# Two score maps in one visit, two value chunks in one visit: a paged decode woven into the dense products of a hybrid decoder step

## The chip, the cores and the metric

The kernel runs on one core of a Trainium2 chip. Time is the device time of the whole program in microseconds (us); less is better. TensorE (PE) does matrix products and transposes, VectorE (DVE) and ScalarE (ACT) elementwise work, GpSimd (POOL) issues the gathers from the page pool, SyncE (SP) most other DMAs. The activations, the weights and the caches come from device memory at the start, and all results are written there.

## The reference

One layer of a decoder for 2048 prompt tokens and for 8 samples of 8 new tokens that each have 8192 cached ones. One projection feeds a gated short convolution and a differential attention; both go through one output projection, and a squared-ReLU MLP follows. The part that the change touches is the attention of the samples over the paged cache:

```python
def sample_attention(q, k, v, lam, k_pool, v_pool, page_table):
    kp = k_pool[page_table].reshape(bd, past, N_HEADS, 2, D_HEAD)    # 8 x 8192 x 4 x 2 x 64
    vp = v_pool[page_table].reshape(bd, past, N_HEADS, D_V)          # 8 x 8192 x 4 x 128
    return diff_attn(q, cat(kp, k), cat(vp, v), past + arange(tn), arange(past + tn), lam)

def diff_attn(q, k, v, q_pos, k_pos, lam):
    s = einsum('bqhcd,bkhcd->bchqk', q, k) * D_HEAD ** -0.5          # c: two score maps
    s = where(dist >= 0, s - slope * dist, NEG)
    p = softmax(s)
    return einsum('bhqk,bkhd->bqhd', p[:, 0] - lam * p[:, 1], v)
```

## The kernel before

**Dense work.** The input projection, the attention of the prompt, the output projection and the MLP are products of 128 x 128 weights with up to 512 columns. Each is made from three passes over split operands (`mm3`, L199 to L201, and L1410 to L1412 for the second MLP product), so three matmuls on TensorE belong together. After such a trio the code calls `between(us)` (L176), the place where other work may be put in.

**Decode.** `decode()` (from L685) is a generator that does the samples' attention in small steps. `tick(us)` (L167) adds the dense work's time to `since` and to a credit, and takes the next step when the credit is positive and `since` has reached the gap that the last step asked for, times 0.7. Each `yield cost, gap` in the generator ends a step. A step's instructions on TensorE, a **visit**, stand thus together between two dense trios. TensorE, like every engine, works through its instructions in the order of the program.

**Rounds.** `rounds()` (from L869) walks over the batches in two phases: the first 2 samples within the input projection (113 to 611 us of the trace), the other 6 within the output projection and the MLP (from about 1143 to 2219 us). A round takes a pair of chunks, 2 x 512 tokens; a sample has 8 rounds. The scores of a round belong to sample b, its values to sample b - 1, so the first 8 rounds of a phase have no values and the last 8, its tail, no keys. In order, a round is:

- scores `sps` (L896 to L908): two maps c, 8 products each of the block-diagonal queries `qbd` with the transposed keys `kt` (16 records in the trace); one step for each map; then DVE adds the bias and takes the maximum (L910);
- `more(n)`: n of the eight transposes of the next round's keys from `kraw` to `kt` on DVE (L717); behind the fourth and the eighth of them (L720 to L723) `gather_k` issues the gather of a later chunk (1 MB, L699); 5 of the 8 stand here, 2 and 1 behind the next steps;
- the exponentials of a round of sample b - 1, the transposes `pps` (L937) of its probabilities, their copies `ptt` on ACT (L940);
- values `o_ps` (L943 to L955): two chunks e, 16 products each (32 records), one step for each chunk; after a chunk's products `gather_v` (L702) issues four gathers of 256 KB for the chunk after next into the buffer `vpg` that this chunk has used. There are two such buffers.

`GP` and `GP2` hold the gaps of a round, for phase one and phase two: `(3, 2, 1, 3, 2, 2, 3, 3)` and `(2, 1, 2, 3, 2, 2, 3, 3)`; `gp()[1]` stands behind the first map, `gp()[0]` behind the second, `gp()[2]` behind the exponentials, `gp()[3]` behind the copies and `gp()[4]`, `gp()[5]` behind the two value chunks. In the code `gp()` takes GP where `b0` is zero. All gathers go through GpSimd's queue in the order in which the code issues them.

Of the kernel before, what the change touches and what calls it, by code (L numbers as in the profile page):

```python
# [20 lines left out]
EPS = 1e-5  # L21
# [45 lines left out]
def tile_hymba_step(  # L67
# [8 lines left out]
    T = x_prompt.shape[1]  # L76
# [59 lines left out]
    def rsqrt(y, v, n, w, eng=None):  # L136
        """y[:n, :w] = v ** -0.5 by Newton's iteration from the exponent trick."""
# [38 lines left out]
    def between(us):  # L176
        """A place between two products where other work of the tensor engine may go."""
        if fillers:
            fillers.pop(0)()
        else:  # L180
            tick(us)
# [15 lines left out]
    def mm3(ps, wh, wl, ah, al, first, last):  # L197
        """ps += (wh + wl)^T (ah + al), all but the product of the two low parts."""
        nc.tensor.matmul(ps, lhsT=wh, rhs=ah, start=first, stop=False)  # L199
        nc.tensor.matmul(ps, lhsT=wh, rhs=al, start=False, stop=False)  # L200
        nc.tensor.matmul(ps, lhsT=wl, rhs=ah, start=False, stop=last)  # L201

    class Weights:
        """Streams [128, 1024] weight tiles and splits each into two float32r parts, ahead of use."""
# [29 lines left out]
        def parts(self):  # L234
            """Closures that split the next tile, a half at a time."""
# [26 lines left out]
        def ahead(self, n):  # L262
            """Splits the next n tiles after those taken."""
# [7 lines left out]
    def norm_sum(x, n, junk=None):  # L271
        """The mean square of each row of x[:n]."""
# [6 lines left out]
    def norm_root(ss, n, eng=None):  # L279
        """(ss + EPS) ** -0.5 for one value a row."""  # L280
# [23 lines left out]
    # order of the column groups of w_in: Q, K, V, then (C, U, B) per convolution group  # L304
# [5 lines left out]
    # the last block ends with Q, whose results leave without a transpose  # L310
# [4 lines left out]
    # token tiles of each block in two chunks of columns: (source, first row, rows, column)  # L315
# [28 lines left out]
    def prep_sum(bi, ci, ss, i):  # L344
        """Sums of squares of a tile of tokens."""
# [17 lines left out]
    def prep_scale(bi, ci, rr):  # L363
        """Closures that normalise a chunk's tokens."""
# [7 lines left out]
    def trans(bi, ci):  # L372
        """Closures that transpose and split a chunk's tokens."""
# [29 lines left out]
    # the first tile's norm by itself  # L403
# [42 lines left out]
    class Proj:  # L446
        """One column group of w_in for one block of tokens."""
# [163 lines left out]
    def proj2(bi, mi):  # L611
        """Two column groups, chunk by chunk: at the ends of a block, where the activations change."""
# [58 lines left out]
    def row_fold(dst, src, op):  # L671
        """dst[(h,g,q), c] = over g: op of src[(h,g,q), c]."""
# [10 lines left out]
    def decode():  # L683
# [28 lines left out]
        def transpose_k(r, t, k):  # L712
            """An eighth of the transposed keys of a pair of chunks."""
# [11 lines left out]
        def load_qc(j):  # L725
            """Queries of four batches."""
# [13 lines left out]
        # page rows: keys in rows of 32 groups of four tokens, values token by token  # L740
# [9 lines left out]
        # bias of a cached key: slope (key - end of its pair of chunks) + slope (that end - query)  # L750
# [31 lines left out]
        # a page's scores and values have token 4 s + j in row 32 j + s  # L782
# [3 lines left out]
        # rows of the scores: (head, page in the group of four, token of the sample)  # L786
# [13 lines left out]
        # lambda on every partition  # L800
# [6 lines left out]
        # rows of the output: (head, map, token) in the first 16 of each 32  # L807
# [7 lines left out]
        # new tokens: column s of group g is token 32 g + s = (batch 4 g + s // 8, s % 8)  # L815
        # distance t - q; allowed where it is not positive
        nc.vector.tensor_scalar(scr[:, 0, :], scr[:, 0, :], rowf[:, 0:1], None, op0=ALU.subtract)
        # owner batch of the column, for this row's group
# [17 lines left out]
        # collects rows (h, c, q) into columns (h, q)  # L836
# [13 lines left out]
        def exps(b, k):  # L850
            """Exponentials of a batch's eighth k of the cached keys; NPR: of the new keys."""
# [8 lines left out]
        def more(n):  # L860
            """Some more of the next pair's transposed keys."""
# [6 lines left out]
        def rounds():  # L868
            """The pairs of chunks of batches b0 to b1."""  # L869
# [14 lines left out]
            for r in range(b0 * NPR, N_PR + NPR):  # L884
# [3 lines left out]
                if r < N_PR:  # L888
# [7 lines left out]
                    # scores of this pair of chunks of four pages  # L896
                    sps = dps.tile([P, 2, 256], F32, tag="sps", bufs=DPB - 1, name="sps")
                    for c in range(2):
# [9 lines left out]
                        yield 1.05, gp()[0] if c else gp()[1]  # L908
# [10 lines left out]
                if pb >= 0:  # L919
# [23 lines left out]
                    yield 0.4, gp()[3]  # L943
                    for e in range(2):
# [10 lines left out]
                        if it + 2 < b1 * NCH:  # L955
                            gather_v(it + 2)
                        more(MO[3 + e])
                        yield 1.2, gp()[4 + e]
# [80 lines left out]
        # sub-norm of the sample tokens: sums over the partitions by a product with ones  # L1039
# [59 lines left out]
    # units in groups of about four chunks of keys  # L1099
# [9 lines left out]
    # loads by the iteration after which they are issued  # L1109
# [11 lines left out]
    def attention_first():  # L1121
        """The attention's first tiles, ahead of the input projection's end."""
# [7 lines left out]
        # key - query position for the last query block; masked past the diagonal  # L1130
# [1021 lines left out]
```

## Time and profile before

| | |
|---|---|
| device time, median of 3 runs (range) | 3255.04 us (3251.31 to 3256.69) |
| span of the profiled execution | 3153.6 us |
| between the median and that span | 101.4 us |
| TensorE busy | 3014.2 us (96%) |
| VectorE / ScalarE / GpSimd busy | 58% / 39% / 28% |
| decode on TensorE, first to last | 112.9 to 2217 us, with a pause for the prompt's attention |

The profile is of one execution; the results give no device time for it besides its span, so the span stands for it and the 101.4 us are what lies around it. A timeline row tells the start, the length and the form of an instruction or of a run of like ones; matmuls overlap, so a group's cost is read from start to start, not from the sum of lengths. In the records a value product of the code stands as two, and so does a score product. An idle time in brackets names what ended it.

### The profile page before, as it was taken

The page shows a single profiled execution, that of the slowest core. Times are in us where ns is not written, and L with a number is a line of the kernel's source. Part 1 is how long each engine was busy: PE and PEld are TensorE (multiplying, and loading weights), DVE is VectorE, ACT ScalarE, POOL GpSimd, SP SyncE. Part 2 cuts the span into 40 slices and gives each one's busy share as a digit, 9 for nine tenths or more (in the row PEclk, how much of TensorE's full clock was granted, in tenths as well). Part 3 has the DMA queues.
Part 4 walks back from the last instruction along what each step waited for, and adds up shares of the span by engine and source line. Part 5 has one row for each costly group of instructions (what it writes and reads, how often), then busy time and mean ns, then how long its engine had stood idle before and what let it go on. Part 6 is the DMA issues. An engine that isn't in the chain of part 4 may idle for free. (4 is left out here: it accounts for less than half of the span.)

```text
span 3153.6 us, 53285 instructions
## 1 busy us (share of the span) xinstructions
PE 3014.2 (96%) x20902; PEld 2532.3 (80%) x20902; DVE 1824.8 (58%) x3751; ACT 1243.3 (39%) x2705; POOL 891.8 (28%) x1266
## 2 busy tenths in 40 slices
PE   7999998999999989999999999999999999999998
PEld 7988887989997788777677777777887788888886
DVE  5376353268888668766676776663653444444444
ACT  3323323357778643333343333343332332222222
POOL 0013355211122121455466564467002010000002
PEclk9999999999999999999999999999999999999999
DMA  4777876754335457899689899677741112111111
GB/s 149 229 232 247 286 255 200 223 140 113 108 99 146 139 176 242 278 320 334 229 288 360 304 347 328 211 274 263 230 145 41 61 54 67 47 54 47 54 47 64
DMA packets 400821, 585.80 MB, mean 186 GB/s; under 512 B 35413, under 2 KB 299605, under 8 KB 384186
## 3 DMA queue, kind: packets, MB, share of 16 engines
q1 hardware_dynamic: 337418, 301.07, 31.1%
q0 software_dynamic: 61984, 277.91, 24.5%
q8 instruction: 165, 2.70, 0.3%
q10 hardware_dynamic: 1168, 3.41, 0.3%
q14 instruction: 86, 0.70, 0.1%
HBM read 526.56 MB, written 55.74 MB: 185 GB/s over the span
## 5 line engine op out<-in xcount | busy, mean ns | idle before, releaser
L707 POOL DMA_INDIRECT vpg<-in_cache_v_dram,pt x512 | 537.5, 1050 | 232.3 <-issue 134.4
L226 ACT CAST wh<-wraw 128x1024 fp32r<-128x1024 f32 x336 | 350.0, 1048 | 632.2 <-PE dps L1412 277.1
L228 DVE TENSOR_TENSOR wl<-wraw,wh 128x1024 fp32r<-128x1024 f32 x336 | 410.2, 1221 | 236.4 <-ACT wh L226 227.4
L199 PE MATMUL ups<-h2h,wh 128*128 128x384 f32 (+2 forms) x1264 | 462.6, 366 | 4.9 <-DVE x L1417 2.5
L1417 DVE TENSOR_TENSOR x<-dps,x 128x512 f32<-128x512 f32 (+1 forms) x528 | 355.2, 684 | 177.2 <-PE dps L1412 176.7
L1410 PE MATMUL dps<-wh,uh 128*128 128x512 f32 (+1 forms) x1076 | 438.8, 408 | 13.2 <-ACT wh L226 5.6
L201 PE MATMUL ups<-h2h,wl 128*128 128x384 f32 (+2 forms) x1264 | 448.8, 355 | 0.0
L200 PE MATMUL ups<-h2l,wh 128*128 128x384 f32 (+2 forms) x1264 | 447.9, 354 | 0.0
L1411 PE MATMUL dps<-wl,uh 128*128 128x512 f32 (+1 forms) x1076 | 425.5, 395 | 4.3 <-DVE wl L228 3.3
L1412 PE MATMUL dps<-wh,ul 128*128 128x512 f32 (+1 forms) x1076 | 424.2, 394 | 0.0
L199 PE MATMUL ps<-hh,wh 128*128 128x384 f32 (+1 forms) x1152 | 404.6, 351 | 1.1 <-ACT cc L1526 0.7
L201 PE MATMUL ps<-hh,wl 128*128 128x384 f32 (+1 forms) x1152 | 376.5, 327 | 3.1 <-DVE wl L228 3.1
L200 PE MATMUL ps<-hl,wh 128*128 128x384 f32 (+1 forms) x1152 | 376.0, 326 | 0.1
L1369 DVE TENSOR_TENSOR ul<-r,uh 128x384 fp32r<-128x384 f32 (+2 forms) x158 | 93.6, 592 | 438.5 <-ACT uh L1368 438.3
L717 DVE STREAM_TRANSPOSE kt<-kraw 128x512 f32<-128x512 f32 x512 | 316.9, 678 | 5.4 <-DMA kraw<-in_cache_k_dram,idxk 5.4
L699 POOL DMA_INDIRECT kraw<-in_cache_k_dram,idxk x128 | 129.1, 1009 | 565.6 <-DVE kt L717 522.8
L199 PEld LDWEIGHTS ups<-h2h,wh 128*128 128x128 f32 x1264 | 238.5, 189 | 54.4 <-issue 28.7
L1410 PEld LDWEIGHTS dps<-wh,uh 128*128 128x128 f32 (+1 forms) x1076 | 200.8, 187 | 85.8 <-issue 24.1
L1366 ACT ACTIVATE r<-ups 128x384 f32<-128x384 f32 (+2 forms) x158 | 82.8, 524 | 445.0 <-PE ups L201 445.0
L200 PEld LDWEIGHTS ups<-h2l,wh 128*128 128x128 f32 x1264 | 238.9, 189 | 16.6
L201 PEld LDWEIGHTS ups<-h2h,wl 128*128 128x128 f32 x1264 | 238.5, 189 | 15.3
L284 POOL TENSOR_SCALAR ss<-ss 128x1 f32<-128x1 f32 (+1 forms) x33 | 9.5, 289 | 839.5 <-ACT junk L276 838.7
(275 smaller groups left out, 4985.8 us busy)
## 6 DMA issues: line engine op xcount, KB each, us to landing
wraw<-in_w_up_dram SPq DMA_DIRECT2D x128, 512.0 KB, 5.0
wraw<-in_w_down_dram SPq DMA_DIRECT2D x128, 512.0 KB, 3.3
wraw<-in_w_in_dram SPq DMA_DIRECT2D x72, 512.0 KB, 4.4
wraw<-in_w_out_dram SPq DMA_DIRECT2D x32, 512.0 KB, 4.2
x<-in_x_prompt_dram SPq DMA_DIRECT2D x24, 512.0 KB, 7.0
vpg<-in_cache_v_dram,pt POOLq DMA_INDIRECT x512
qt<-QH SPq DMA_DIRECT2D x64, 128.0 KB, 4.5
qt<-QL SPq DMA_DIRECT2D x64, 128.0 KB, 5.0
```

The source lines that it names most:

```text
L199: nc.tensor.matmul(ps, lhsT=wh, rhs=ah, start=first, stop=False)
L200: nc.tensor.matmul(ps, lhsT=wh, rhs=al, start=False, stop=False)
L201: nc.tensor.matmul(ps, lhsT=wl, rhs=ah, start=False, stop=last)
L226: nc.scalar.copy(wh, t)
L228: eng.tensor_sub(wl, t, wh.bitcast(F32))
L699: nc.gpsimd.indirect_dma_start(out=t.rearrange("p a b -> p (a b)"), out_offset=None, in_=ck, in_offset=bass.IndirectOffsetOnAxis(ap=idxk[: ...
L707: nc.gpsimd.indirect_dma_start(out=t[:, g, :], out_offset=None, in_=cv, in_offset=bass.IndirectOffsetOnAxis(ap=idxv[:, 4 * it + g:4 * it + ...
L717: nc.vector.transpose(t[:, e, 16 * j:16 * j + 16].rearrange("p a b -> p (a b)"), kraw[2 * r + e][:, 16 * j:16 * j + 16].rearrange("p a b - ...
L1410: nc.tensor.matmul(ps, lhsT=uh, rhs=wh[:, half], start=(i == 0), stop=False)
L1411: nc.tensor.matmul(ps, lhsT=uh, rhs=wl[:, half], start=False, stop=False)
L1412: nc.tensor.matmul(ps, lhsT=ul, rhs=wh[:, half], start=False, stop=(i == len(ms) - 1))
L1417: nc.vector.tensor_add(xx, ps, xx)
```

## The change

The two maps of a round's scores are made in one step with the gap that stood behind the second; the gap that stood behind the first is added to the one ahead of the values. The two chunks of values are made in one step with the sum of their gaps; their gathers are issued behind both. The rest of the diff takes comments away; line numbers from L956 on are higher by one after it.

```diff
                     for c in range(2):
                         for db in range(2):
...
-                        yield 1.05, gp()[0] if c else gp()[1]
+                    yield 2.1, gp()[0]
...
                     more(MO[2])
-                    yield 0.4, gp()[3]
+                    yield 0.4, gp()[3] + gp()[1]
                     for e in range(2):
                         it = NCH * pb + 2 * i + e
                         v = vpg.pop(it)
...
-                        if it + 2 < b1 * NCH:
-                            gather_v(it + 2)
+                    for e in range(2):
+                        if NCH * pb + 2 * i + e + 2 < b1 * NCH:
+                            gather_v(NCH * pb + 2 * i + e + 2)
                         more(MO[3 + e])
-                        yield 1.2, gp()[4 + e]
+                    yield 2.4, gp()[4] + gp()[5]
```

How the instructions stand then is shown at three places. The first is TensorE at the scores of one round of phase two, whose keys are `kt` and queries `qbd`; `dps` is a dense product of the MLP. Before:

```order
L902 MATMUL sps_15857<-kt_15729,qbd_14450 32x256 x8
L1410 MATMUL dps_15852<-wh_15717,uh_15527 128x512
L1411 MATMUL dps_15852<-wl_15718,uh_15527 128x512
L1412 MATMUL dps_15852<-wh_15717,ul_15528 128x512
L1410 MATMUL dps_15870<-wh_15640,uh_15450 128x512
L1411 MATMUL dps_15870<-wl_15641,uh_15450 128x512
L1412 MATMUL dps_15870<-wh_15640,ul_15451 128x512
L902 MATMUL sps_15857<-kt_15729,qbd_14450 32x256 x8
```

The same scores after:

```order
L1412 MATMUL dps_15716<-wl_15582,uh_15373 128x512
L1413 MATMUL dps_15716<-wh_15581,ul_15374 128x512
L902 MATMUL sps_15724<-kt_15599,qbd_14368 32x256 x16
L1411 MATMUL dps_15742<-wh_15483,uh_15293 128x512
L1412 MATMUL dps_15742<-wl_15484,uh_15293 128x512
L1413 MATMUL dps_15742<-wh_15483,ul_15294 128x512
```

The two visits with two dense trios between them have become one visit of 16 products.

The second place is TensorE at the values of a round of phase two; `ptt` holds the probabilities, `vpg` the gathered values of one chunk, and `ps` and `ups` are dense. Before:

```order
L949 MATMUL o_ps_13174<-vpg_14918,ptt_15055 16x128 x16
L1410 MATMUL dps_15105<-wh_14858,uh_14651 128x512
L1411 MATMUL dps_15105<-wl_14859,uh_14651 128x512
L1412 MATMUL dps_15105<-wh_14858,ul_14652 128x512
L1410 MATMUL dps_15105<-wh_14930,uh_14714 128x512
L1411 MATMUL dps_15105<-wl_14931,uh_14714 128x512
L1412 MATMUL dps_15105<-wh_14930,ul_14715 128x512
L199 MATMUL ups_15119<-h2h00_12958,wh_15019 128x384
L200 MATMUL ups_15119<-h2l00_12960,wh_15019 128x384
L201 MATMUL ups_15119<-h2h00_12958,wl_15020 128x384
L949 MATMUL o_ps_13174<-vpg_14962,ptt_15055 16x128 x16
```

The same values after:

```order
L200 MATMUL ups_14949<-h2l01_12961,wh_14823 128x384
L201 MATMUL ups_14949<-h2h01_12959,wl_14824 128x384
L949 MATMUL o_ps_13174<-vpg_14861,ptt_14963 16x128 x16
L949 MATMUL o_ps_13174<-vpg_14866,ptt_14963 16x128 x16
L199 MATMUL ups_15042<-h2h00_12958,wh_14913 128x384
L200 MATMUL ups_15042<-h2l00_12960,wh_14913 128x384
```

The products of the second chunk follow those of the first, and the three dense trios that stood between them stand outside.

The third place is GpSimd's queue in a round of phase two, its two key gathers and the first six of its eight value gathers, with the engines and DMA queues that an instruction waits for (PE is TensorE, DVE VectorE, DMASW a queue of gathers). Before:

```order
L699 DMA kraw<-in_cache_k_dram,idxk 128x2048 [waits DMASW4_49,DVE_49]
L699 DMA kraw<-in_cache_k_dram,idxk 128x2048 [waits DMASW5_49,DVE_49]
L707 DMA vpg<-in_cache_v_dram,pt 128x512 [waits DMASW7_49,DMASW6_49,PE_49]
L707 DMA vpg<-in_cache_v_dram,pt 128x512
L707 DMA vpg<-in_cache_v_dram,pt 128x512 [waits DMASW0_49]
L707 DMA vpg<-in_cache_v_dram,pt 128x512 [waits DMASW1_49]
L707 DMA vpg<-in_cache_v_dram,pt 128x512 [waits DMASW3_49,DMASW2_49,PE_49]
L707 DMA vpg<-in_cache_v_dram,pt 128x512
```

And after:

```order
L699 DMA kraw<-in_cache_k_dram,idxk 128x2048 [waits DMASW2_49,DVE_49]
L699 DMA kraw<-in_cache_k_dram,idxk 128x2048 [waits DMASW3_49,DVE_49]
L707 DMA vpg<-in_cache_v_dram,pt 128x512 [waits DMASW5_49,DMASW4_49,PE_49]
L707 DMA vpg<-in_cache_v_dram,pt 128x512
L707 DMA vpg<-in_cache_v_dram,pt 128x512 [waits DMASW6_49]
L707 DMA vpg<-in_cache_v_dram,pt 128x512 [waits DMASW7_49]
L707 DMA vpg<-in_cache_v_dram,pt 128x512 [waits DMASW1_49,DMASW0_49,PE_49]
L707 DMA vpg<-in_cache_v_dram,pt 128x512
```

The order and the kinds of the waits are the same: two key gathers that wait for DVE, then the value gathers, of which the first and the fifth wait for PE. What moved is TensorE's instruction behind which these waits end.

## Rows read from the trace of the kernel before

**Rows 1.** Page, part 1: busy time, share of the span, instructions of each engine.

```profile
PE 3014.2 (96%) x20902; PEld 2532.3 (80%) x20902; DVE 1824.8 (58%) x3751; ACT 1243.3 (39%) x2705; POOL 891.8 (28%) x1266
```

**Rows 2.** Tile answers, score and value products: ns min/median/max, first and last start, forms.

```profile
L902 PE MATMUL sps<-kt,qbd x2048: 376/379/637, 112.9 to 2092.7; 128*32 128x256 f32 x187
...
L949 PE MATMUL o_ps<-vpg,ptt x4096: 269/273/421, 299.9 to 2211.8; 128*16 128x128 f32 x196
```

**Rows 3.** Timeline of TensorE, one score visit: start us, us, operation, tile, count.

```profile
1301.12 0.33 PE L200 MATMUL ups<-h2l,wh 128*128 128x384 f32 x1
1301.29 0.34 PE L201 MATMUL ups<-h2h,wl 128*128 128x384 f32 x1
1301.56 1.07 PE L902 MATMUL sps<-kt,qbd 128*32 128x256 f32 x16
...
1302.85 0.34 PE L200 MATMUL ups<-h2l,wh 128*128 128x384 f32 x1
```

**Rows 4.** Timeline of TensorE, one value visit.

```profile
2012.34 0.34 PE L201 MATMUL ups<-h2h,wl 128*128 128x384 f32 x1
2012.61 1.07 PE L949 MATMUL o_ps<-vpg,ptt 128*16 128x128 f32 x32
...
2013.88 0.34 PE L200 MATMUL ups<-h2l,wh 128*128 128x384 f32 x1
```

**Rows 5.** Waits of TensorE, whole span: us in total, times, longest.

```profile
PE o_ps L949 <- DMA vpg<-in_cache_v_dram,pt: 20.7, 25, 2.3
...
PE o_ps L949 <- ACT ptt L940: 13.3, 6, 5.0
```

**Rows 6.** Timeline of GpSimd's queue in the second tail; in brackets the idle time before.

```profile
2123.23 0.98 POOL L707 DMA_INDIRECT vpg<-in_cache_v_dram,pt  x1 [6.40 <-PE o_ps L949]
...
2133.34 1.43 POOL L707 DMA_INDIRECT vpg<-in_cache_v_dram,pt  x1 [0.30 <-issue]
```

**Rows 7.** Timeline of TensorE in the same tail, value visits of two rounds.

```profile
2121.86 1.07 PE L949 MATMUL o_ps<-vpg,ptt 128*16 128x128 f32 x32
...
2132.15 1.07 PE L949 MATMUL o_ps<-vpg,ptt 128*16 128x128 f32 x32
...
2135.62 0.41 PE L949 MATMUL o_ps<-vpg,ptt 128*16 128x128 f32 x8
...
2139.09 0.63 PE L949 MATMUL o_ps<-vpg,ptt 128*16 128x128 f32 x8 [1.85 <-DMA vpg<-in_cache_v_dram,pt]
```

**Rows 8.** Timeline of TensorE, rounds with key gathers: two score visits, one late value group.

```profile
1727.07 1.07 PE L902 MATMUL sps<-kt,qbd 128*32 128x256 f32 x16
...
1755.26 0.41 PE L949 MATMUL o_ps<-vpg,ptt 128*16 128x128 f32 x8 [1.29 <-DMA vpg<-in_cache_v_dram,pt]
...
1822.17 1.07 PE L902 MATMUL sps<-kt,qbd 128*32 128x256 f32 x16
```

**Rows 9.** Timeline of GpSimd's queue in the same two rounds.

```profile
1741.83 0.94 POOL L699 DMA_INDIRECT kraw<-in_cache_k_dram,idxk  x1 [2.03 <-DVE kt L717]
1743.08 1.61 POOL L707 DMA_INDIRECT vpg<-in_cache_v_dram,pt  x1 [0.30 <-issue]
...
1747.50 0.95 POOL L707 DMA_INDIRECT vpg<-in_cache_v_dram,pt  x1 [0.30 <-issue]
...
1752.50 1.00 POOL L707 DMA_INDIRECT vpg<-in_cache_v_dram,pt  x1 [0.31 <-issue]
...
1830.67 1.92 POOL L699 DMA_INDIRECT kraw<-in_cache_k_dram,idxk  x1 [0.30 <-issue]
```

**Rows 10.** Windows: us, busy PE, PEld, DVE, ACT, POOL, granted clock, DMA share, GB/s.

```profile
1700.00:1930.00 230.00, 226.66 (x2162) 174.21 (x2164) 167.41 (x319) 86.86 (x181) 140.27 (x133) 1.00 0.94 332
...
2139.50:2142.50 3.00, 3.00 (x13) 2.33 (x8) 1.16 (x2) 0.00 (x0) 2.17 (x3) 0.55 0.72 246
```

**Rows 11.** Waits of TensorE between 2096 and 2215 us, the second tail.

```profile
PE o_ps L949 <- DMA vpg<-in_cache_v_dram,pt: 6.0, 7, 1.9
```

**Rows 12.** Waits of TensorE between 1200 and 2090 us, phase two with key gathers.

```profile
PE o_ps L949 <- DMA vpg<-in_cache_v_dram,pt: 8.5, 11, 1.5
```

## The prediction, made before the changed kernel ran

> **What bounds the kernel now.** I read the page's table of busy times first: TensorE is busy 3014.2 of 3153.6 us, 96%, and the next engine, VectorE, 58% [rows 1]. So a microsecond taken from TensorE's own work is a microsecond of the end, unless something that TensorE waits for moves out by as much. Then I read the two tiles of the decode: 2048 score products and 4096 value products, in bodies that are much shorter in pitch than the dense products around them [rows 2]. Third, the timeline of one score visit and one value visit: before and after each there is a gap that belongs to no product [rows 3, 4]. Fourth, the list of waits: value products wait for the gathered values 20.7 us in all and for the copied probabilities 13.3 us [rows 5]. That is little, and it says that the value gathers land just in time. Whether they still do is what decides this change, so I then read when they are issued and when they are used, in the rounds without key gathers [rows 6, 7] and in those with them [rows 8, 9], and how full the DMA engines are [rows 10].
>
> **What the change removes: 64 + 64 visits.** A score visit of one map: from the last dense product before it to the second one after it 1302.85 - 1301.29 = 1.56 us [rows 3]. Two dense pitches of 0.173 (1301.29 - 1301.12) would have passed anyway, so the visit costs 1.21. Its body: the group of 16 records takes 1.07 from the first start to the last end, one record lasts 0.379 [rows 2, 3], so 15 pitches take 0.69 and a pitch is 0.046; 16 of them are 0.74. What is left, 0.47, is the price of going in and out. A value visit: 2013.88 - 2012.34 = 1.54 [rows 4], less 0.35 is 1.19; its body 32 x (1.07 - 0.27)/31 = 0.82; in and out 0.37. The order shows 64 score visits and 64 value visits where there were 128 each, the same products in them and the same dense products around them. That a second half in the same visit pays nothing at its start is read from the same groups: each changes its head, and with it the columns of the array that it uses, from product to product, and has no gap inside [rows 3, 4]. Saved, if TensorE is what binds: 64 x 0.47 + 64 x 0.37 = 30 + 24 = **54 us**.
>
> **What it moves: the value gathers.** TensorE's dense work per round gets shorter in the order, not only the visits: with the gaps written as they are, a round of phase two holds 10.0 us of dense products instead of 10.7 (counted in the order, at the pitches of the rows), since four gaps of a round are rounded up to the next place between products in place of six. That gives nothing by itself, for the dense work is the same; decode is only over some 41 us of dense work sooner. But the gathers of a round have less time. On POOL nothing is reordered: two key gathers, then eight value gathers; the first and the fifth of these wait for TensorE to let go of a buffer, the key gathers for VectorE. The fifth now waits for the one merged visit, together with the first.
>
> *Rounds without key gathers* (the tails of the two phases, 14 intervals). Before: the first gather is issued 1.37 us after the start of the first chunk's visit (2123.23 - 2121.86), the others follow at 1.25 where nothing holds them ((1752.50 - 1747.50)/4, [rows 9]), so the eighth comes about 9 us after the first (2133.34 - 2123.23 = 10.1 here, where another DMA is put between) [rows 6, 7]. Its data are used 2139.09 - 2133.34 = 5.75 us after its issue, in a visit that waited for them. Together the last group is ready 1.4 + 9 + 5.7 = 16.1 us after the visit began. It is wanted in the next round's second visit, 3.5 us (2135.62 - 2132.15) after that round's first, and the first visits are 10.1 to 10.3 us apart (2132.15 - 2121.86 = 10.29 with its waits). So the waits of two neighbouring rounds add to 16.1 - 3.6 - 10.1 = 2.4, 1.2 a round; the list has 6.0 us for the seven rounds of the second tail [rows 11], 0.9 a round, and the working holds. After: last group wanted 1.44 into the merged visit, period 10.6 (by the order 8.3 us of dense work in place of 7.8, one visit less): 16.1 - 1.4 - 10.6 = 4.1, 2.0 a round. That is 0.85 x 14 = **+12 us**.
>
> *Rounds with key gathers* (38 rounds of phase two). Here the value gathers stand behind the second key gather, and that behind the transpose of the keys on VectorE. Its lag behind the start of the last score product is 14.1 in one round (1727.07 + 0.69 to 1741.83) and 7.8 in another (1822.17 + 0.69 to 1830.67) [rows 8, 9]; over 37 of the 38 rounds it lies between 6.3 and 16.3, mean 10.9 (the last holds a pause, 32.9). The last group is ready lag + 1.25 + 9.1 + 5.7 = lag + 16.05 after that product (1743.08 to 1752.50 is 9.4 for the seven steps). Before, it is wanted 7.0 + 16.1 + 3.6 = 26.7 after it: waits of two rounds add to lag - 10.7, about nothing, and the list has 8.5 us in eleven waits for the 40 rounds [rows 12] (read as the lengthening of the visits in those rounds, restarts and waits for the probabilities included, it is 14 us, 0.35 a round, and that I take). After, by the order, the value visit starts 7.65 after the last score product, the period without waits is 16.1 - 0.85 - 0.7 = 14.5, and the last group is wanted 1.44 into the visit: 23.6. The waits of two rounds add to lag - 7.55 = 3.35, 1.7 a round if the lag stays. The other end: the stretch from 1700 to 1930 moves 332 GB/s with the DMA engines 0.94 busy [rows 10], that is 5.35 MB a round of 16.1 us; at full share 353 GB/s, 15.1 us a round, so at least 0.65 of waiting against 14.5. Each wait gives VectorE time to catch up and shortens the lag, which speaks for less than 1.7. I take 1.2, in the middle: (1.2 - 0.35) x 38 = **+32 us**; the ends are +11 and +51.
>
> By the Trainium skill ("HBM Reference", "Specifications (TRN2)") a core that streams alone reaches about 425 GB/s, and the floor of such a round would be an estimated 12.6 us, no floor at all against 14.5. The stretch shows 332 GB/s at 0.94 of the engines' time, and the row decides.
>
> **Two small terms.** The gap before the value visit takes over the dropped one (2 in phase one, 1 in phase two, times 0.7): the six waits for the probabilities of 13.3 us [rows 5] lose up to 0.7 to 1.4 each, **-4**. After a longer wait the clock falls: behind the wait of 1.85 us that ends at 2139.09 [rows 7] the granted clock is 0.55 for 3 us, near the lower of its two levels of 1.2 and 2.4 GHz [rows 10]. Such a dip costs 3 x 0.45 = 1.4 us; I take three more of them, **+4** (0 to 20).
>
> **Sum.** -54 + 12 + 32 - 4 + 4 = -10. Made on the profiled execution: its span of 3153.6 becomes 3143.6. The median of the runs, 3255.04, lies 101.4 above that span, which I leave as it is: **3245 us**.
>
> **The rivals.** *A, the full gain.* Lag and landing both shrink, because shorter rounds let VectorE work on the keys sooner in the order; at a lag of 7.5 the waits in key rounds come to nothing, -54 + 12 - 13 = -55, and where they stay as they are, -42: 3200 to 3213. For it: lags of 6.3 to 8 are there in several rounds [rows 9]; against: the mean is 10.9, and the DMA share leaves 6%. By the Trainium skill ("DMA: Bandwidth & Descriptors", "Anatomy of one DMA — SWDGE (gpsimd) path") a transfer takes 2.0 us and its bytes over 436 GB/s, an estimated 2.6 us for a gather of 256 KB; that is 3.1 less than the 5.75 of the row, the waits of two rounds in key rounds would come to about 0.2, and the page's rule ends in this rival. The row shows the longer time under load.
>
> *B, slower.* In each key round the loop value visit, release, eight gathers, landing binds: the lag stays at 10.9 and the waits at 1.7 a round. Then -54 + 12 + 51 - 4 + 4 = +9, 3264. Dips of the clock behind ten more of these waits add 14; and where the landing is longer, as for the fourth gather of a round, whose group of eight records started 1755.26 - 1747.50 = 7.8 us after its issue with a wait ahead of it [rows 8, 9], a round waits another 1.0, which in eight of the 38 rounds is 8: 3286 with both. So 3262 to 3285. It decides from a lag of about 9.5 upward, at which the waits, 1 a round, and the clock eat the gain. For it: the mean lag is above that. Against: in a round that waits VectorE gains on TensorE.
>
> *C, cancelled.* Waits and saving meet within 0.2%, 6.5 us: lag near 10 with few dips. 3248.5 to 3261.5.
>
> *D, it doesn't do what it says.* The merged visits' second half pays as much as a visit did. Then nothing is saved, and the waits still come: 3255 + 44 = 3299. Against it stands the even pitch of rows 4; 0.03.
>
> **How the numbers follow.** A difference under 0.2% (6.5 us) can hardly be told from none. Forecast (saving partly eaten, 3215 to 3248.5): 0.37. A: 0.15. C: 0.20. B: 0.25, D 0.03. Faster 0.52, same 0.20, slower 0.28. Eight in ten: from the middle of A to the upper end of B, 3205 to 3285; the faster cases alone run from 3200 to 3248.5.
>
> **What would show it.** Right: the tile answers show groups of 32 score records and 64 value records at the same pitches, decode ends about 40 us sooner, and the list of waits has value products waiting for gathers some 60 to 80 us in place of 20.7, mostly in phase two. A: that line stays near 20 to 30. B: above 90, with stretches of half clock behind them. The forecast is wrong if the lag of the second key gather changes by more than 2 us, or if the last group lands in under 4 or over 7 us in key rounds.

## The result, and the profile after

| | before | after |
|---|---|---|
| device time, median | 3254.59 us (3251.31 to 3256.69) | 3329.57 us (3323.87 to 3335.75) |
| after to before | | 1.0248, 95% interval 1.0217 to 1.0278 |
| predicted | | 3245 us, range 3205 to 3285 |

The change makes the kernel 75 us slower, and 3330 lies above the range. One fact is needed to read the rest: the runs were made on several chips, and the unchanged kernel takes 3150 to 3154 us on three of them and 3251 to 3255 on the others; they are called quick and slow chips here. In every later profile the device time is about 2 us above the span. So the first profile of the kernel before (span 3153.6) must be from a quick chip, while the times beside it are from a slow one, and the 101.4 us that the prediction let lie "around the span" were the difference of two chips. Ratios below are always against the kernel before on the same chip; where a trace of a slow chip stands beside one of a quick chip, it is said.

The profile after (a slow chip). First line: busy times of the page, as in [rows 1].

```profile
PE 3067.9 (92%) x20902; PEld 2589.6 (78%) x20902; DVE 1818.2 (55%) x3751; ACT 1242.7 (37%) x2705; POOL 880.6 (27%) x1266
```

TensorE has fallen from 96% to 92%; part of that is the chip, for the 96% are from a quick one. One merged score visit and one merged value visit, as in [rows 3, 4]:

```profile
1460.30 0.34 PE L201 MATMUL ups<-h2h,wl 128*128 128x384 f32 x1
1460.57 1.93 PE L902 MATMUL sps<-kt,qbd 128*32 128x256 f32 x32
...
1462.71 0.33 PE L200 MATMUL ups<-h2l,wh 128*128 128x384 f32 x1
...
1491.72 0.34 PE L201 MATMUL ups<-h2h,wl 128*128 128x384 f32 x1
1491.99 1.94 PE L949 MATMUL o_ps<-vpg,ptt 128*16 128x128 f32 x64
...
1494.14 0.34 PE L200 MATMUL ups<-h2l,wh 128*128 128x384 f32 x1
```

From the last dense product to the second one behind the visit: 1462.71 - 1460.30 = 2.41 us for the scores, less two pitches of 0.173 is 2.06, where two visits cost 2 x 1.21; saved 0.36. The values: 1494.14 - 1491.72 = 2.42, 2.07, where two visits cost 2 x 1.19; saved 0.31. So 64 x 0.67 = 43 us of TensorE's own work are saved, not 54: inside the visits a seam stays, for the scores (1.93 - 0.38) - 2 x 0.69 - 0.05 = 0.12 us, for the values (1.94 - 0.27) - 2 x 0.80 - 0.03 = 0.04. The visits do what the change says. The waits of TensorE over the whole span, as in [rows 5] (us, times, longest):

```profile
PE o_ps L949 <- DMA vpg<-in_cache_v_dram,pt: 37.1, 40, 3.2
PE dps L1412 <- DVE wl L228: 23.6, 13, 6.5
...
PE o_ps L949 <- issue: 16.0, 33, 1.1
PE sps L902 <- issue: 12.5, 21, 1.0
...
PE sps L902 <- DVE kt L717: 8.3, 6, 3.7
```

Value products wait for gathers 37.1 us where the first profile, of a quick chip, had 20.7. New beside them are the low parts of the weights (`wl`, 3.3 us there for the same line), the keys (1.7 there) and gaps for which the trace has no cause ("issue"), 66.0 us in 118 places over all of TensorE's lines; the first profile has none of these last ones, nor has any other trace of the kernel before on a quick chip. The same list for the stretch with key gathers alone (1357 to 2194 us), TensorE's first three lines:

```profile
PE dps L1412 <- DVE wl L228: 16.4, 7, 6.5
PE o_ps L949 <- issue: 12.1, 24, 1.1
PE o_ps L949 <- DMA vpg<-in_cache_v_dram,pt: 11.2, 18, 1.7
```

In these rounds the prediction expected most of its new waits, but value products wait for gathers only 11.2 us there (8.5 before, [rows 12]). All listed waits in this stretch are 103 us, of which 40 are "issue" and 23 are for weights. And the clock of the same stretch:

```profile
1356.78:2193.79 837.01, 732.72 (x6484) 566.70 (x6483) 510.89 (x944) 272.96 (x554) 428.06 (x467) 0.95 0.79 279
```

The granted clock over the stretch with key gathers is 0.95, its DMA share 0.79, at 279 GB/s: the engines for transfers were idle more, not less, than in the kernel before on a quick chip (0.94 and 332 GB/s in [rows 10], 0.87 and 305 GB/s over the whole such stretch, shown below).

### The profile page after: what moved, and what is told of

It reads as the page before. It is cut to its first block, busy times and chain, and to the rows that moved or that the text cites. A ratio compares the mean times of both kernels' runs of the same rounds, so it can differ in the third digit from the quotient of the medians.

```text
span 3322.1 us, 53272 instructions
## 1 busy us (share of the span) xinstructions
PE 3067.9 (92%) x20902; PEld 2589.6 (78%) x20902; DVE 1818.2 (55%) x3751; ACT 1242.7 (37%) x2705; POOL 880.6 (27%) x1266
## 4 chain that ended last, share of the span: by engine, by line
PE 35%; issue 8%; DVE 6%; POOL 6%; DMA 5%; another core or an unknown queue 2%; ACT 1%; POOLq 0%; DVEq 0%; ACTq 0%
PE dps L1413 5%; PE dps L1411 5%; PE dps L1412 5%; PE ups L199 5%; PE ups L201 5%; PE ups L200 5%; POOL vpg L707 4%; DVE kt L717 2%; DMA kraw<-in_cache_k_dram,idxk 1%; DVE wl L228 1%; DMA vpg<-in_cache_v_dram,pt 1%; DMA wraw<-in_w_out_dram 1%; PE o_ps L949 1%; PE ps L1301 1%
## 5 line engine op out<-in xcount | busy, mean ns | idle before, releaser
L707 POOL DMA_INDIRECT vpg<-in_cache_v_dram,pt x512 | 522.5, 1020 | 279.8 <-issue 141.9
L1412 PEld LDWEIGHTS dps<-wl,uh 128*128 128x128 f32 (+1 forms) x1076 | 203.3, 189 | 77.0 <-DVE wl L228 32.7
```

The costliest lines, as they stand in the source:

```text
L707: nc.gpsimd.indirect_dma_start(out=t[:, g, :], out_offset=None, in_=cv, in_offset=bass.IndirectOffsetOnAxis(ap=idxv[:, 4 * it + g:4 * it + ...
L1412: nc.tensor.matmul(ps, lhsT=uh, rhs=wl[:, half], start=False, stop=False)
```

## The experiments

Two theories went in. **L**: the value gathers, released together by the merged visit, land too late. **I**: a run of 64 short records outruns TensorE's supply of instructions, which makes the "issue" gaps. A third, **P**, came after the first four runs: the rounds stand closer together in the dense work, and that costs by itself. The expectations also name **T**: the traffic of the closer rounds makes weights, keys and values all come late.

**The kernel before again, and the change again**

> The kernel before, unchanged, to see what lies between the 3153.6 us of its first profile and its timed 3254.6 us. The profile after shows a span only 1.8 us below its device time. Theory S (the first profile was of a quicker execution than the timed ones): span within 5 us of about 3252, and TensorE gaps that nothing in the profile explains ('issue'), of which the first profile has none and the profile after has 66 us, now 30 us or more. Theory O (the 100 us lie around the span): span about 3154 again and no such gaps.

> The kernel before, for a profile on the chip of the next three. Where it takes some 3150 us, its waits are those of the first two profiles (value products for gathers 15 to 25 us, no gaps without a cause); where it takes some 3250, the 100 us are to be found: gaps on TensorE that nothing explains, 40 us or more, and longer waits for gathers, in a kernel whose visits are the short ones.

> The kernel before, for its trace beside the merged one's on one chip. On a chip where it takes some 3250 us: if the unexplained gaps are the chip's and not the change's, they are there with the short visits too, 30 us or more in the rounds with key gathers (the merged kernels have 30 to 40); if they come from the long visits, under 10.

> The changed kernel again, beside the kernel before and the next three on one chip. If the loss does not depend on the chip, the ratio is 1.02 to 1.03 again (3210 to 3240 where the kernel before takes 3150). The profile tells which waits are the change's own: value products for gathers 45 to 75 us, and hardly any of the gaps that nothing explains, of which its first trace has 66 us.

Measured: the kernel before 3137.4, 3143.5 and 3148.4 us, with spans 1.8 us below, on three quick chips; none of its traces has a gap without a cause, and there is no trace of it from a slow chip. Neither theory S nor theory O of e1 came out as written: that chip was quick in its timed runs too. The changed kernel again on a slow chip: 3325.6 us, 1.0234 (1.019 to 1.0279), so the ratio stands. Its trace has the "issue" gaps again, 66.7 us, against the expectation of hardly any.

**One half alone**

```diff
# e2_score
-                        yield 1.05, gp()[0] if c else gp()[1]
+                    yield 2.1, gp()[0]
...
-                    yield 0.4, gp()[3]
+                    yield 0.4, gp()[3] + gp()[1]
# e3_value: the value part of the change alone
# e4_gap0: e2_score, and
-                        yield 1.2, gp()[4 + e]
+                        yield 1.2, gp()[4] + gp()[5] if e else 0.0
```

> Only the two score maps in one visit (and their gap ahead of the values); values as before. Theory L (late value gathers make the loss): values are wanted much as before, so the saving of 64 x 0.47 = 30 us comes out, less the 0.126 us that the seam between the maps costs in the trace after (8 us): 3225 to 3240. Theory I (a run of 64 short records outruns TensorE's supply of instructions): the score part of the gaps in the visits stays, 29 us by the trace after, and the dips of the clock behind them: 3255 to 3280.

> Only the two value chunks in one visit; scores as before. Theory L: it holds nearly the whole loss, 75 us, plus the 22 us that the score merge would have saved: 3320 to 3355. Theory I: the value visits hold 128 records of which some 16 us of unexplained gaps were seen, so it has about half of the loss: 3275 to 3310.

> Scores merged as in the change; the two value chunks stand one dense trio apart (gap 0), each followed by its own gathers. The values are wanted only some 1 us later than in the change and released as early, but no value visit is longer than before. Theory L: the waits for gathers stay within 10 us of the change, time 3315 to 3350. Theory I: only the score half of the gaps is left, time 3270 to 3300.

Measured on a quick chip (before 3150.0): scores alone 1.0111 (1.0094 to 1.0127), values alone 1.0209 (1.0188 to 1.0230), values one dense trio apart 1.0156 (1.012 to 1.0192). Waits of TensorE, two lines of the score run, then three of the value run:

```profile
PE o_ps L949 <- DMA vpg<-in_cache_v_dram,pt: 26.5, 45, 2.5
...
PE dps L1411 <- DVE wl L228: 10.5, 10, 2.9
```

```profile
PE o_ps L949 <- DMA vpg<-in_cache_v_dram,pt: 64.9, 84, 5.2
...
PE o_ps L949 <- ACT ptt L940: 11.3, 6, 8.8
...
PE ops L984 <- DVE osc L981: 9.9, 1, 9.9
```

The value half has the waits that theory L named, 64.9 us against 16.6 in the kernel before on that chip, and its loss of 70 us is in L's range. The run with the values one trio apart, 50 us lost, lies between the two expectations. There is not one unexplained gap in the value run and 0.2 us in the score run, so theory I falls on this chip as a cause: the loss is there without it. But the score half loses 35 us where theory L expects 22 gained: something is missing in both.

**The pace**

```diff
# e7_pace_only: the kernel before, with
-                        yield 1.05, gp()[0] if c else gp()[1]
+                        yield 1.05, gp()[0] if c else 0.0
# e6_pace, e16_pace, e18_pace: the changed kernel, with
-                    yield 2.1, gp()[0]
+                    yield 2.1, gp()[0] + (0 if pb >= 0 else gp()[1])
...
-                    yield 0.4, gp()[3] + gp()[1]
+                    yield 0.4, gp()[3] + (gp()[1] + 1.0 if r < N_PR else 0.5)
# e8_score_pace: e2_score, with the first of these lines and
-                    yield 0.4, gp()[3] + gp()[1]
+                    yield 0.4, gp()[3] + (gp()[1] + (0.7 if b0 else 0) if r < N_PR else 0)
```

> Nothing merged: the kernel before, with gap 0 behind the first score map, so that the rounds hold as much dense work as in the run with merged scores alone (480.8 us against 481.3 over the rounds with key gathers, 503.3 before). Theory P: as slow as that run and slower by its saved visits, 35 to 60 us over the kernel before, 3185 to 3210. Theory L: the values are wanted 0.5 us sooner in a round, 10 us or less: 3145 to 3162.

> Both merges as in the change, but gaps widened until the rounds hold as much dense work as before (503.9 us against 503.3 over the rounds with key gathers, by the order; 471.8 in the change; decode ends at the same place as before). Theory P (a round with key gathers takes its time whatever dense work stands in it, so the work that the change pushes out of the rounds is paid behind them): the loss goes and the merge pays, 64 x 0.34 + 64 x 0.32 = 42 us less than before, 3105 to 3130 against 3150. Theory L (the values are wanted too soon behind their release, which the merge moved): the waits for gathers stay at 40 us or more, 3165 to 3200.

> Score maps merged, values as before, gaps widened until the rounds hold as much dense work as before (501.9 us). Both theories: the visits saved, 64 x 0.34 = 22 us: 3122 to 3140. Where it stays at 3150 or above, the merged score visit has a price of its own (what it holds up on VectorE, or the run of short records), and neither theory has the whole cause.

> The merged kernel at the old dense pace again, beside the three others: 0.998 to 1.006 if the chip does not matter. On a chip where the kernel before takes 3150 us its trace tells without the unexplained gaps where the 42 us of saved visits went: waits of TensorE in the rounds with key gathers 20 to 40 us above the kernel before's 31 to 36 (theories L and T), or none, and then its visits cost more than the timelines said.

> The merged kernel at the old dense pace. If the unexplained gaps hide its saving, it comes out on a chip that has none: 0.985 to 0.993 of the kernel before there, and 1.000 to 1.006 on the others. If gathers and weights eat it (theory T), it is 0.998 to 1.006 on any chip, with 20 to 40 us more waits in the rounds with key gathers than the kernel before.

Measured: with nothing merged and the rounds closer (22 of the 31 us of dense work that the change takes out of the stretch), 1.0141 (1.0096 to 1.0187), 49 us lost, as theory P said. With both merges and the rounds as far apart as before: 1.002 (1.000 to 1.004), 1.0044 (1.0016 to 1.0071) on two slow chips, 1.0055 (1.0037 to 1.0073) on a quick one. Scores merged at the old pace: 1.001 (0.9991 to 1.003). The changed kernel (e5) and e6 differ by the pace alone, on one chip: 3325.6 and 3259.0 us, 67 us apart. So the pace has most of the loss. But theory P's other half, that the merge then pays, failed in all four runs: at the old pace it returns none of its 43 us, and by e8's own sign neither P nor L has the whole cause. The last trace tells where the 43 us went. The stretch of the 39 rounds from the first score visit beside values to the last one, first of the kernel before, then of the merged kernel, both on one quick chip; the columns are those of [rows 10]:

```profile
1302.77:2079.80 777.03, 743.93 (x6649) 567.35 (x6648) 537.63 (x980) 291.79 (x582) 444.66 (x484) 0.98 0.87 305
```

```profile
1302.16:2092.61 790.45, 732.76 (x6654) 582.25 (x6654) 530.34 (x968) 291.92 (x582) 444.34 (x481) 0.97 0.85 301
```

And in that stretch the first two waits of the kernel before and the first three of the merged one:

```profile
PE o_ps L949 <- DMA vpg<-in_cache_v_dram,pt: 7.2, 9, 2.1
PE o_ps L949 <- ACT ptt L940: 6.9, 5, 3.9
```

```profile
PE o_ps L949 <- DMA vpg<-in_cache_v_dram,pt: 21.1, 40, 1.5
PE dps L1412 <- DVE wl L228: 6.8, 6, 2.3
PE dps L1411 <- ACT wh L226: 5.8, 2, 4.2
```

TensorE is busy 11 us less (743.93 to 732.76) at a lower clock, and idle more: for gathers 21.1 us for 7.2, for weights 21 for 7 over all lines. What the visits give is taken by waits and by the clock behind them. The unexplained gaps are not in it: this chip has none. The table sets the stretch of each kernel beside the dense work that it holds (counted in the order of instructions, 0.173 us for 384 columns); the rest should have fallen by 13 us for each half that is merged. The last column is the time from the last value product to the end of the trace, in which nearly all work is dense. Rows e1 to e3 are of one chip, e5 to e7 of another.

| kernel, chip | stretch, us | dense work in it | rest | after decode |
|---|---|---|---|---|
| before (e17), quick | 777 | 503 | 274 | 942 |
| before (e1), quick | 776 | 503 | 273 | 941 |
| scores merged (e2), quick | 782 | 481 | 301 | 968 |
| values merged (e3), quick | 815 | 489 | 326 | 963 |
| both, old pace (e18), quick | 790 | 504 | 286 | 944 |
| both, half of the values (e12), quick | 716 | 472 | 244 | 982 |
| nothing merged, farther apart (e11), quick | 856 | 561 | 295 | 874 |
| both, farther apart (e10), quick | 869 | 574 | 295 | 873 |
| both (after), slow | 837 | 472 | 365 | 983 |
| both (e5), slow | 839 | 472 | 367 | 985 |
| both, old pace (e6), slow | 847 | 504 | 343 | 946 |
| nothing merged, closer (e7), slow | 850 | 481 | 369 | 972 |

From e6 to e5, 32 us of dense work leave the stretch: it gets 8 us shorter, and what follows decode gets 39 us longer.

**Less traffic**

```diff
# e12_half_v: the changed kernel, with
-                        gather_v(b0 * NCH + 1)
...
-                        v = vpg.pop(it)
+                        v = vpg.pop(it) if e == 0 else v
...
-                        if NCH * pb + 2 * i + e + 2 < b1 * NCH:
+                        if e == 0 and NCH * pb + 2 * i + e + 2 < b1 * NCH:
# e14_half_k: the changed kernel; kraw[2 * r] is transposed for both chunks,
-            if j == 3:
+            if k == 7:
...
-                    gather_k(2 * r + e + 2)
+                    gather_k(2 * r + 4)
```

> The changed kernel at its own dense pace, but only the first chunk of each pair of value chunks is gathered and both products read it (half of the value gathers left out). Its buffers are then free a round ahead. Theory P: no wait for value gathers, and some 60 to 100 us less than the changed kernel: 0.99 to 1.005 of the kernel before. Rival I: instructions are the same on TensorE, so the loss stays: 1.015 to 1.025.

> The changed kernel with half of the key gathers left out (both halves of the keys are transposed from the first chunk's data; the others are not fetched). Value gathers are all there and wait for the same visits, but the engines have 1 MB a round less to move, and the queue of GpSimd one gather less ahead of them. Theory T: the loss goes as with half of the value gathers, 0.985 to 1.000. Theory L: it shrinks by the 1.25 us and the shorter landing only, 1.005 to 1.018.

Measured: half of the value gathers, 0.990 (0.9879 to 0.992), on a quick chip; half of the key gathers, 1.0124 (1.0053 to 1.0195), on a slow one. Each leaves out 1 MB a round. The first, with a buffer a round ahead, comes near what the prediction's rival A forecast for the change (0.983 to 0.987 of the kernel before):

```profile
1291.29:2007.52 716.23, 682.07 (x6483) 551.80 (x6482) 510.39 (x945) 273.67 (x554) 277.79 (x319) 0.99 0.77 270
```

The clock is back at 0.99, and the rest in the table falls by 30 us, where 26 were due. Half of the keys bring back about half of the loss, in the range that theory L expected; traffic alone (theory T of the expectation) would have brought all of it. But the gain did not come on theory L's way: value products wait for gathers 43.0 us in that trace, as in the changed kernel (37.1 and 43.6).

**The queue's order**

```diff
# e13_defer on the changed kernel, e15_pace_defer on e6_pace
-                    gather_k(2 * r + e + 2)
+                    if e and r - 1 >= (b0 + 1) * NPR:
+                        late_k.append(2 * r + e + 2)
+                    else:
+                        gather_k(2 * r + e + 2)
...
                             gather_v(NCH * pb + 2 * i + e + 2)
+                        if late_k:
+                            gather_k(late_k.pop())
```

> The changed kernel with one gather moved on GpSimd's queue: the second key gather of a round stands behind the first four value gathers, not ahead of them. Traffic and TensorE's instructions are the change's; the value gathers are issued up to 3 us sooner after their buffer is free, the second key gather later. Theory L (the loss is the lateness of the value gathers): waits for gathers fall to 20 us or less and the loss of 1.024 shrinks by a third or more: 1.005 to 1.016. Theory T (the loss is the traffic of the shorter rounds: weights, keys and values all come late): 1.020 to 1.028, with the waits moved to the keys or the weights.

> The merged kernel at the old dense pace (1.002 of the kernel before) with the second key gather behind the first four value gathers. Theory L: the waits that ate the saving were the values', 0.990 to 0.998, a version that beats both. Theory T: 0.998 to 1.006.

Measured: 1.0277 (1.0219 to 1.0334) and 1.0092 (1.0057 to 1.0127), no better than without, 1.0234 and 1.0044. The queue of GpSimd in one round of the first:

```profile
1813.26 0.97 POOL L700 DMA_INDIRECT kraw<-in_cache_k_dram,idxk  x1 [8.15 <-DVE kt L718]
...
1815.12 0.98 POOL L708 DMA_INDIRECT vpg<-in_cache_v_dram,pt  x1 [0.30 <-issue]
1816.41 1.95 POOL L708 DMA_INDIRECT vpg<-in_cache_v_dram,pt  x1 [0.31 <-issue]
1818.66 0.95 POOL L708 DMA_INDIRECT vpg<-in_cache_v_dram,pt  x1 [0.30 <-issue]
1819.91 0.95 POOL L708 DMA_INDIRECT vpg<-in_cache_v_dram,pt  x1 [0.30 <-issue]
1821.16 0.94 POOL L700 DMA_INDIRECT kraw<-in_cache_k_dram,idxk  x1 [0.30 <-issue]
1822.41 0.95 POOL L708 DMA_INDIRECT vpg<-in_cache_v_dram,pt  x1 [0.30 <-PE dps L1419]
```

The second key gather stands behind four value gathers as meant. In the mean of 37 rounds the first value gather is issued 2.5 us after the start of the value visit instead of 5.0, yet the eighth lands 19.2 us after it, as without the move (read from the completions of the gathers' queue in the DMA records): it still stands behind both key gathers, is issued 0.9 us sooner and takes 0.9 us longer to land. Here theory T's number came out. What falls is the plain form of theory L, that the second key gather's place in the queue makes the loss; since the last data came no sooner, the run doesn't test whether their lateness does. Taken with the half of the keys, neither theory has it all.

**A slower pace**

```diff
# e10_merged_slow on e6_pace, e11_before_slow on the kernel before
-GS = (0.7, 0.7, 0.7)
+GS = (0.7, 0.7, 0.82)
```

> Both merges, and the gaps of the second phase longer still (times 0.82 for 0.7): 574 us of dense work over the rounds with key gathers for 503 before, decode over at 1624 us of dense work for 1527. Theory P (gathers set the time of a round; dense work in it is free until they are covered): waits for gathers under 15 us and the visits saved (42 us) come out at last, 0.975 to 0.990 of the kernel before. Rival I (the merged visit has its own price, gaps inside it): as in the run with the old pace, 0.998 to 1.006.

> The kernel before, nothing merged, with the same longer gaps (561 us of dense work over those rounds). Theory P: the waits of the kernel before go, but no visit is saved: 0.985 to 0.998. Where it gains as much as the run with merged visits, merging is worth nothing even where the gathers are in time.

Measured: 1.0136 (1.0103 to 1.0169) and 1.0093 (1.0074 to 1.0112). Theory P as written here falls: more dense work in the rounds isn't free, the rest in the table rises to 295 us in both. What follows decode gets 69 and 68 us shorter, but the stretch gets 92 and 79 us longer. Part of the loss is a wait behind decode. In both kernels decode ends so late that what comes behind it, the last group of tokens, meets its first weights unsplit; a wait of the merged one between 2290 and 2460 us:

```profile
PE ps L1300 <- ACT wh L226: 25.4, 1, 25.4
```

The other has one of 18.1 us there, the kernel before one of 2.6. Why the rest rises I have not traced. No version that reads all keys and values beats the kernel before.

## Why the prediction was wrong

**What TensorE saves** was right in kind, and its term was 54 us for a measured 43; the seams were not in it. Rival D (nothing saved) is out.

**The step that failed** is the sentence that the shorter rounds give "nothing by itself, for the dense work is the same". The prediction saw the 0.7 us a round in the order and took it out of the period, but priced only how much sooner the last value group is wanted. That term was put at nothing; with nothing merged, closer rounds alone cost 1.4% or 49 us (e7), and with both merges the pace alone is worth 67 us (e6 to e5). While all values are gathered, the rounds with keys hardly get shorter when work is taken out of them: their stretch lasts 776 us with 503 us of dense work in it, 782 with 481 and one half merged, 815 with 489 and the other. The work that leaves them is paid after decode, which is the last column of the table. Decode was forecast to end 40 us sooner; on the quick chip of e1 to e3 it ends 15 and 65 us later with one half merged.

**The term for key rounds**, +32 with ends at +11 and +51, priced only waits for gathered values. For the whole change these waits came out smaller: 11.2 us in the stretch (14.3 in e5) for 6 to 9 in the traces of the kernel before. The value half alone has 34.0 (e3), 28 more than the kernel before on that chip, near the forecast. Three things were wrong in it.

- The lag of the second key gather did not shrink under the waits, as argued ("each wait gives VectorE time to catch up"). On quick chips its mean (37 rounds, the longest left out) is 10.6 to 10.9 us in the kernel before and 10.8 to 11.7 with one half or both merged (e2, e3, e4, e18). It is 13.1 in the trace after, but that is a slow chip, and there it is 13.0 with nothing merged (e7). By the prediction's own formula 13.1 would give 2.8 us of waiting a round and a term of +93, which the list doesn't show, so the formula fell too.
- Other waits, for weights, for keys and for the scaled output (`osc`), were not priced: in the trace after the value gathers are 37.1 of 241.9 us of listed waits over the whole span, between the prediction's signs for rival A (20 to 30) and for its forecast (60 to 80).
- The clock: +4 was taken; in the value run it stands at 0.95 over the stretch for 0.98 before, by estimate 0.03 x 740 = 22 us.

**Rival B** had the right side, and its loop (value visit, release, eight gathers, landing) didn't get shorter. It takes 18.6 to 20.1 us in the mean from the start of a value visit to the landing of its eighth gather, in all kernels with full value gathers, however they are arranged, 19.1 before and 19.2 after. Before, the last of these data are wanted in a second visit, some 3.9 us into the next one; merged, 1.5 us into it. That takes over two us a round of slack away, and the closer rounds another 0.7. That this loop holds the rounds is borne out by the waits of the value half alone. For the whole change it is argued and not shown: its rounds wait little for gathers, and those of e7, which loses 49 us, wait 4.8 us. B's price of 3262 to 3285 left out the pace and was too low. That the two value buffers, used up at once, act like one deep buffer is how I read it; the run with half of the value gathers, in which a buffer is a round ahead, agrees, but it also takes traffic away, and the runs don't part the two.

**Tails**: +12 was taken. On quick chips the first tail took 116 to 119 us before and 119 to 123 in the runs with one half or both merged (e2, e3, e18), the second 84 to 89 before and 92 to 95; the size was about right. **Probabilities**: -4 was taken; they fall from 9.9 to 1.1 us in e18 and from 10.8 to 7.8 in e2, but are 19.0 in e16, the kernel of e18 on a slow chip. So the sign is not settled.

**Rival A and the two places of the Trainium skill.** The rule of the Trainium skill ("DMA: Bandwidth & Descriptors", "Anatomy of one DMA — SWDGE (gpsimd) path") ended in rival A, by an estimated landing of 2.6 us. The eighth gather of a round landed 4.9 us after its issue in the mean of 37 rounds of the kernel before; the measurement decides. The Trainium skill ("HBM Reference", "Specifications (TRN2)") has about 425 GB/s for a core that streams alone. The rounds with key gathers (the 29 to 31 without pauses) show 326 GB/s in the mean at a share of 0.93 before (e17, quick) and 293 at 0.83 after (slow). Neither comes near that rate, and the rounds were not held by the rate alone, since it fell.

**What stays open.** The whole change ran on slow chips only (1.0248 and 1.0234); on quick ones its halves did (1.0111 and 1.0209). How the loss splits between late value gathers, traffic and clock is not settled, nor what keeps the rounds from getting shorter in the whole change and in e7, nor what makes the "issue" gaps.

## What to carry to other kernels

Taking work out of an engine that is 96% busy pays only where that engine is what a stage waits for; ask what the stage's loop over its buffers takes, and set the wanted moment of its last datum beside it. Two users of a two-deep buffer that are put together may take its depth away; here that is a reading, not shown by itself. When an edit also moves the pace at which background work is woven in, run the pace alone: here it was worth more than the edit.

## What the runs showed of the hardware

Chips differ: the same kernel takes 3150 to 3154 us on three and 3251 to 3255 on the others; each was met on one occasion only. On the slow ones TensorE has gaps that nothing in the profile explains, 46 to 67 us in each of nine traces, in bursts of short products most of all, but in dense products too; in the stretch with keys they are 40 us in all for the change and 38 with nothing merged (e7). The first four lines of these 38, waits of TensorE:

```profile
PE o_ps L949 <- issue: 16.5, 12, 5.4
PE sps L902 <- issue: 4.9, 8, 0.8
PE ups L199 <- issue: 2.8, 7, 0.7
PE dps L1410 <- issue: 2.6, 6, 0.9
```

In the eleven traces of quick chips there are 0.2 us at most. These gaps are smaller than the 100 us between the chips; where the rest lies is open. On quick chips a run of 32 short score records and one of 64 value records pass at the plain pitch, but for the seam in the middle.
